# Matmul and DMA prices of a build-time scheduler, changed to the durations in the trace

## The chip, the cores and the metric

The kernel runs on one core of one Trainium2 chip. The metric is the device time of one execution in microseconds (us). TensorE is called PE here, VectorE DVE, ScalarE ACT, GpSimd POOL and SyncE SP. SP and POOL mainly issue DMA transfers.

## What is computed

The reference is a two-layer trunk over 528 tokens (16 learned meta tokens in front of 512 others), width 1024, all in float32. Cut to what matters:

```python
for l in range(DEPTH):                                   # DEPTH = 2
    n = rms_norm(h, mix_norm_g[l])
    # n @ w_in[l] is split by columns into q, k, v, qi, ki, wi (attention),
    # xr, yg (recurrent branch), c (convolution branch) and the merge gates
    logits = einsum("bqhd,bsd->bqhs", qi, ki)            # the indexer, 8 heads of 64
    iscore = einsum("bqhs,bqh->bqs", relu(logits), wi)
    _, sel = lax.top_k(iscore, 128)                      # each query keeps 128 keys
    p = softmax(q @ ksel * scale); o = p @ vsel          # 8 heads of 128, 2 key heads
    # recurrent branch: 4-tap conv, gates, scan, gelu
    # conv branch: GLU, 31-tap causal depthwise conv, layer norm, silu
    # three output projections, merge by sigmoid gates, w_out, residual
    # rms norm, SwiGLU feed-forward (2816 wide), residual
```

## The kernel before

**Tiles and passes.** Activations lie transposed in SBUF, as tiles `s` of 128 channels by 528 tokens. A product in float32 is made of three passes in a rounded format: weights and activations are each split into a rounded part (hi) and the rest (lo). `gemm` (from L539) first multiplies the hi weights with the activations' hi and lo (L568, the hi pass), then the lo weights with the activations' hi (L578, the lo pass). One output tile of 128 channels takes 32 matmuls of 264 columns at L568 and 16 at L578 in layer 0, and half as many of 512 columns in most of layer 1. The feed-forward and one projection use a scheme of seven products (`seven`, L609 and L613).

**The way of a weight.** SP loads 512 KB of raw weights (L397). ACT writes the rounded hi copy into a `w` slot, later a negated lo copy into another, and POOL issues a DMA that adds the raw weights from memory onto it (L400, `add_dma`). There are four `w` slots.

**The stages of a layer.** The norm; the product for the values (`v_gemm`, L891), whose first matmuls reuse a PSUM bank that DVE reads into `rtok` (L386, the reciprocal norms by token, used by the indexer); the indexer (`choose`), whose top-k runs on DVE as 16 rounds of MAX and MATCH_REPLACE over each of four score tiles (L1003 and L1004); rotations of q, k and the indexer's q (`rotate`: two POOL transfers that swap halves inside SBUF, s<-s, and three DVE operations at L379); then eight heads. A head is: scores on PE (L953, L962), a softmax (DVE at L1234, Exp on ACT, a reciprocal on DVE at L1237, a scaling on ACT), transposes of the probabilities on PE (L1325) and their product with the values (L1346). The 31 taps of the conv branch are DVE operations at L382 on tiles of about 512 elements; they need only their input tile. All through the stage the large products of the projection run on PE.

**What sets the order.** The kernel is written as some dozens of Python generators, and `Sched.run` (from L213) interleaves them when the program is built. Each yields an `Op` with an engine and a price in ns. `start` gives the time at which an op could start by the prices; `run` takes the op with the earliest start (within 40 ns by priority), emits it, and moves that engine's clock on. The outcome is one fixed queue of instructions for each engine, which the chip works through strictly in order, waiting on semaphores: the prices set an order and nothing else. A matmul's price is its columns over about 2.34 per ns; a transfer lands, by the plan, at the time its bytes have gone through a common pipe of 360 bytes per ns, plus `MOVE_LAT`, 1900 ns.

The names in the order's rows (`s_405`, `w_15414`) are numbered anew in each program; the text says which tiles they are.

Of the kernel before, what the change touches and what calls it, by code (L numbers as in the profile page):

```python
# [117 lines left out]
TABLES = {"Exp": ("e",), "Tanh": ("e", "g", "s"), "Gelu_apprx_tanh": ("g",), "Silu": ("s",), "Sqrt": ("q",),  # L118
          "Abs_reciprocal_sqrt": ("a",)}
TABLE_LOAD = 1283.0  # L120
MOVE_LAT = 1900.0
SELF = {"PE": 0.0, "DVE": 125.0, "ACT": 110.0, "SP": 0.0, "POOL": 0.0}
LAT = {"PE": 170.0, "DVE": 100.0, "ACT": 130.0, "SP": 0.0, "ACTQ": 0.0, "POOL": 0.0}

# [1 line left out]
class Sched:  # L126
# [80 lines left out]
    def run(self):  # L207
        while self.streams:
            moved = True
            while moved:  # L210
                moved = False
                for s in sorted(self.streams, key=lambda s: s[:2]):
                    r = s[3]  # L213
                    if isinstance(r, Box):
                        if r.done:
                            self.step(s, r.v)
                            moved = True
                            break
                    elif isinstance(r, Alloc) and r.kind in ("pp", "b1"):
                        b = self.bank(r.kind, r.keep)  # L220
                        if b is not None:
                            self.step(s, b)
                            moved = True
                            break
                    elif isinstance(r, Alloc):
                        free = self.slots[r.kind]
                        if len(free) >= r.n + (r.keep() if callable(r.keep) else r.keep):
                            got = []
                            for dt in r.dts:
                                at, i = heapq.heappop(free)  # L230
                                b = Buf(r.kind, i, self.make(r.kind, i, dt))
                                b.rd = at + 60.0
                                got.append(b)
                            self.step(s, got if r.many else got[0])
                            moved = True
                            break
            cands = []
            for s in self.streams:
                if isinstance(s[3], Op):
                    ready, t = self.start(s[3])  # L240
                    pen = max(0.0, TABLE_LOAD * (PEN_S if s[3].tab == ("s",) else PEN) - AGE * (t - ready)) if s[3].tab and self.table not in s[3].tab else 0.0
                    cands.append((t + pen, s, t))
            if not cands:
                if not self.streams:
                    return
                raise RuntimeError("nothing can go on: " + ", ".join(
                    f"{s[2].__name__}:{s[3].kind + str(s[3].n) if isinstance(s[3], Alloc) else 'box'}" for s in self.streams))
            first = min(cands, key=lambda c: c[0])
            e, until = first[1][3].eng, first[0] + WINDOW
            t0, s, t = min((c for c in cands if c[1][3].eng == e and c[0] <= until), key=lambda c: c[1][:2])  # L250
            op = s[3]
            cost = op.cost
            if op.tab:
                if self.table not in op.tab:
                    self.table = op.tab[0]
                    cost += TABLE_LOAD
            op.fn()
            end = t + cost
            self.clock[e] = end
            done = end  # L260
            if op.bytes:
                self.moved = max(self.moved, end + 650.0) + op.bytes / 360.0
                done = self.moved + MOVE_LAT
            for b in op.R:
                b.rd = max(b.rd, done + LAT[e])
            for b in op.W:
                b.ready, b.eng = max(b.ready, done), e
            self.step(s, None)
# [10 lines left out]
def trunk(ctx, tc, xT, wt, wv, wd, wg, gain_in, par_in, cst_in, id_in, out):  # L279
    nc = tc.nc  # L280
    V, S, PE = nc.vector, nc.scalar, nc.tensor
# [108 lines left out]
        return Op("DVE", cost, fn, R, W)  # L390

    def pe(cost, fn, R, W):
        return Op("PE", cost, fn, R, W)

    def dma(o, i, R, W, q="SP"):
        e = {"SP": nc.sync, "POOL": nc.gpsimd}[q]
# [157 lines left out]
    def gemm(wbox, nk, xs, cols, epi, prio, need="", keep=0, tail=0, ks=range(NF)):  # L554

        n = cols[1] * cols[2]
        bufs = (yield alloc(need, FT, keep)) if need else []
        hi = yield wbox[0]
        ps = yield psa(cols)
        cuts = [0, nk - tail, nk] if tail < nk else [*range(nk + 1)]  # L560
        for k0, k1 in zip(cuts[:-1], cuts[1:]):
            for k in ks[k0:k1]:
                xh, xl = yield xs[k]

                def go(k=k, xh=xh, xl=xl):
                    for i, b in enumerate((xh, xl)):
                        for o, x in by_part(ps, b, cols):
                            PE.matmul(o, hi[:, 128 * k:128 * k + 128], x, start=(k == ks[0] and i == 0), stop=False)  # L568
                yield pe(2 * n / 2.336, go, [hi, xh, xl], [ps])
            if k1 == nk and k0 < k1:  # L570
                free(hi)
            lo = yield wbox[1]
            for k in ks[k0:k1]:
                xh, _ = xs[k].v

                def go(k=k, xh=xh):
                    for o, x in by_part(ps, xh, cols):
                        PE.matmul(o, lo[:, 128 * k:128 * k + 128], x, start=False, stop=k == ks[nk - 1])  # L578
                yield pe(n / 2.336, go, [lo, xh], [ps])
        free(lo)  # L580
        spawn(epi(ps, psv(ps, cols), *bufs), prio)

    def seven(wb, qs, cols, epi, prio, need):
# [7 lines left out]
        for i in (1, 6, 2, 7, 5, 4, 3):  # L591
            wh, wl = yield wb[i]
            if i in (6, 5):
                pair[i] = pair[{6: 2, 5: 4}[i]] = yield Alloc("b1" if near else "pp")
            ps = pair[i] if i in pair else (yield Alloc("b1"))
            if i in pair:
                h = int(i in (6, 5))
                d = ps[:, h * n:h * n + n] if near else ps[:, h, :n]
            else:
                d = ps[:, :n]  # L600
            q = []
            for c in range(4):
                q.append((yield qs[c])[i])
            R = [t for x in q for t in x[:2]]

            def hi(w=wh, d=d, q=q):
                for c, (h, l, o) in enumerate(q):
                    for e, t in enumerate((h, l)):
                        PE.matmul(d, w[:, 128 * c:128 * c + 128], t[:, o:o + n], start=c == 0 and e == 0, stop=False)  # L609

            def lo(w=wl, d=d, q=q):
                for c, (h, l, o) in enumerate(q):
                    PE.matmul(d, w[:, 128 * c:128 * c + 128], h[:, o:o + n], start=False, stop=c == 3)  # L613
            yield pe(8 * n / 2.336, hi, R + [wh], [ps])
            yield pe(4 * n / 2.336, lo, R + [wl], [ps])
            free(wh, wl)
            done[i].set((ps, d))
# [1150 lines left out]
```

## Time and profile before

| | |
|---|---|
| median of three runs | 2175.06 us (2170.46 to 2175.31) |
| profiled execution | 2181.13 us, its span 2179.3 us |
| PE busy | 2103.5 us, 97% |
| DVE busy | 1587.6 us, 73% |
| ACT busy | 1364.8 us, 63% |
| mean granted PE clock | 0.991 of full |

PE is busy in all but some 76 us of the span, so the view to read is what PE waits for. The other engines have a lower share over the whole span, but not in every stretch: DVE's share is near 0.9 in the attention stages (about 78 to 360 us and 1165 to 1440 us) and lower elsewhere. Every time below is in us from the start of the span.

### The profile page before, as it was taken

To read this page: it belongs to the slowest core of one execution; us is meant where nothing else is said; L and a number is where in the kernel's file an instruction comes from. 1 tells how busy PE (TensorE), PEld (TensorE's weight loads), DVE (VectorE), ACT (ScalarE), POOL (GpSimd) and SP (SyncE) were. 2 spreads that over 40 slices of the span, in tenths; PEclk is the share of its full clock that TensorE was granted. 3 is DMA by queue.
4 is the path that set the end of the run, shared out by engine and by line. 5 is a ranking of instruction groups with operands and counts; after the bars stand their busy time and mean duration, and the time that the engine had idled before them with its cause. 6 is when DMAs were issued, how large, how long until landed. Compare 5 with 4: busy or idle time off the path is not lost.

```text
span 2179.3 us, 38132 instructions
## 1 busy us (share of the span) xinstructions
PE 2103.5 (97%) x14808; PEld 1974.2 (91%) x14808; DVE 1587.6 (73%) x2990; ACT 1364.8 (63%) x2113; POOL 318.4 (15%) x392
## 2 busy tenths in 40 slices
PE   6989999999999999999999899999999999999999
PEld 6889999999999999999989888988877887899997
DVE  7699987997237487677668999889972465767674
ACT  6556878876565465555457478888765645655452
POOL 1112110111111011111111111111111110111120
PEclk9999999999999999999999999999999999999999
DMA  8468654788887486576466686568888966766563
GB/s 229 101 142 187 144 120 104 172 175 170 174 202 184 120 184 148 131 169 165 103 186 144 148 186 138 122 133 170 181 178 182 214 156 140 181 151 158 148 143 107
DMA packets 127045, 342.68 MB, mean 157 GB/s; under 512 B 14864, under 2 KB 17040, under 8 KB 126864
## 3 DMA queue, kind: packets, MB, share of 16 engines
q0 software_dynamic: 50112, 145.47, 37.6%
q1 hardware_dynamic: 76608, 194.76, 30.7%
q8 instruction: 116, 1.90, 0.3%
q14 instruction: 65, 0.53, 0.1%
q10 hardware_dynamic: 144, 0.02, 0.0%
HBM read 327.91 MB, written 4.26 MB: 152 GB/s over the span
## 4 chain that ended last, share of the span: by engine, by line
PE 68%; DMA 14%; issue 10%; DVE 3%; ACT 3%; POOL 1%; POOLq 0%; DVEq 0%; ACTq 0%
PE banks L568 28%; PE banks L578 16%; DMA w<-in_wt_dram 14%; PE banks L609 11%; PE banks L613 6%; PE banks L1346 1%; PE banks L891 1%; DVE s L379 1%; PE banks L953 1%; PE banks L1325 1%; ACT w L376 1%; ACT s L376 1%; PE banks L962 1%; PE banks L1086 1%; DVE mx L1003 1%
## 5 line engine op out<-in xcount | busy, mean ns | idle before, releaser
L568 PE MATMUL banks<-s,w 128*128 128x264 f32 (+1 forms) x6432 | 1032.6, 313 | 12.8 <-ACT w L376 7.1
L568 PEld LDWEIGHTS banks<-s,w 128*128 128x128 f32 x6432 | 907.5, 190 | 80.8 <-ACT w L376 7.1
L376 ACT ACTIVATE w<-raw 128x1024 fp32r<-128x1024 f32 (+3 forms) x486 | 480.5, 993 | 338.9 <-PE banks L568 131.9
L578 PE MATMUL banks<-s,w 128*128 128x264 f32 (+1 forms) x3216 | 554.3, 317 | 34.0 <-DMA w<-in_wt_dram 33.5
L578 PEld LDWEIGHTS banks<-s,w 128*128 128x128 f32 x3216 | 463.5, 191 | 79.7 <-DMA w<-in_wt_dram 46.5
L376 ACT ACTIVATE s<-s 128x512 fp32r<-128x512 f32 (+8 forms) x640 | 379.7, 614 | 90.4 <-DVE s L379 68.3
L379 DVE TENSOR_TENSOR s<-s,s 128x528 f32<-128x528 f32 (+9 forms) x522 | 329.5, 656 | 59.2 <-ACT s L376 39.5
L379 DVE TENSOR_TENSOR s<-s,banks 128x512 f32<-128x512 f32 (+3 forms) x340 | 195.4, 588 | 225.2 <-PE banks L578 128.4
L400 POOL DMA_DIRECT2D w<-in_wt_dram x192 | 167.2, 871 | 1262.4 <-ACT w L376 1110.7
L382 DVE SCALAR_TENSOR_TENSOR s<-s,half,s 128x512 f32<-128x512 f32 (+22 forms) x480 | 344.0, 745 | 3.6 <-ACT s L376 0.3
L609 PE MATMUL banks<-s,s 128*128 128x264 f32 (+1 forms) x2464 | 346.0, 283 | 0.4 <-DVE s L379 0.3
L609 PEld LDWEIGHTS banks<-s,s 128*128 128x128 f32 x2464 | 317.9, 188 | 2.4 <-DVE s L379 0.8
L376 ACT ACTIVATE s<-banks 128x528 f32<-128x528 f32 (+11 forms) x338 | 165.0, 505 | 127.5 <-PE banks L578 49.0
L376 ACT ACTIVATE s<-u 128x512 fp32r<-128x512 f32 x176 | 110.5, 628 | 182.3 <-DVE u L379 167.1
L613 PE MATMUL banks<-s,s 128*128 128x264 f32 (+1 forms) x1232 | 199.0, 284 | 6.9 <-DMA s<-in_wt_dram 6.9
L400 POOL DMA_DIRECT2D s<-in_wt_dram x132 | 113.8, 862 | 514.1 <-ACT s L376 343.8
L613 PEld LDWEIGHTS banks<-s,s 128*128 128x128 f32 x1232 | 168.9, 188 | 8.7 <-DMA s<-in_wt_dram 7.5
L379 DVE TENSOR_TENSOR s<-u,s 128x512 fp32r<-128x512 f32 x176 | 119.8, 688 | 33.6 <-ACT s L376 31.0
L382 DVE SCALAR_TENSOR_TENSOR s<-s,banks 128x528 f32<-128x528 f32 (+1 forms) x48 | 33.4, 696 | 117.4 <-PE banks L578 117.3
L376 ACT ACT_TABLE_LOAD x80 | 102.6, 1283 | 4.9 <-DMA s<-in_xT_dram 3.6
L379 DVE TENSOR_TENSOR w<-raw,w 128x512 fp32r<-128x512 f32 (+2 forms) x94 | 75.5, 811 | 5.3 <-ACT w L376 4.4
L379 DVE TENSOR_TENSOR u<-s,s 128x512 f32<-128x512 f32 x88 | 60.3, 686 | 24.5 <-DMA s<-in_wt_dram 24.5
(128 smaller groups left out, 1278.9 us busy)
## 6 DMA issues: line engine op xcount, KB each, us to landing
raw<-in_wt_dram SPq DMA_DIRECT2D x206, 512.0 KB, 4.3
w<-in_wt_dram POOLq DMA_DIRECT2D x192, 512.0 KB, 7.7
s<-in_wt_dram SPq DMA_DIRECT2D x176, 256.0 KB, 5.0
s<-in_wt_dram POOLq DMA_DIRECT2D x132, 256.0 KB, 4.5
raw<-in_wd_dram SPq DMA_DIRECT2D x64, 256.0 KB, 3.7
raw<-in_wd_dram SPq DMA_DIRECT2D x16, 384.0 KB, 3.8
s<-s POOLq DMA_DIRECT2D x36, 132.0 KB, 7.3
s<-in_xT_dram SPq DMA_DIRECT2D x16, 264.0 KB, 4.8
```

What stands on the lines that cost most here:

```text
L376: return Op("ACT", cost, lambda: S.activation(o, i, f, **kw), R, W, TABLES.get(name))
L379: return Op("DVE", 69 + width(o) / 0.96, lambda: V.tensor_tensor(o, a, b, op), R, W)
L382: return Op("DVE", (69 if isinstance(s, float) else 129) + width(o) / 0.96, lambda: V.scalar_tensor_tensor(o, a, s, b, op0, op1), R, W)
L400: return Op("POOL", 1040.0, lambda: nc.gpsimd.dma_start(out=o, in_=i, accum_op=ALU.add), R, W, None, 4 * o.shape[0] * width(o))
L568: PE.matmul(o, hi[:, 128 * k:128 * k + 128], x, start=(k == ks[0] and i == 0), stop=False)
L578: PE.matmul(o, lo[:, 128 * k:128 * k + 128], x, start=False, stop=k == ks[nk - 1])
L609: PE.matmul(d, w[:, 128 * c:128 * c + 128], t[:, o:o + n], start=c == 0 and e == 0, stop=False)
L613: PE.matmul(d, w[:, 128 * c:128 * c + 128], h[:, o:o + n], start=False, stop=c == 3)
L891: PE.matmul(ps[:tn, :264], a[:, t0:t0 + tn], b[:, o:o + 264], start=e + part + k == 0 and a is nh, stop=bool(e and part and k == 3))
L953: PE.matmul(ps[:, :w], a, b[:, :w], start=e == 0, stop=e == n - 1)
L962: PE.matmul(ps[:, c, :hw], a, b[:, c * hw:(c + 1) * hw], start=e == 0, stop=e == n - 1)
L1003: yield dve(70 + w / 0.96, lambda: V.max(mx[rows], sv[rows]), [sc], [])
```

## The change

Two prices of the plan are replaced. A transfer's price now depends on the queue that issues it: bytes per ns and a fixed latency of (310, 2000) for SP and ACT, and (210, 4300) for POOL, in place of 360 and 1900 for all. The price of every PE op is multiplied by 1.066. Prices of DVE and ACT operations, of issuing a DMA (470 ns on SP, 1000 or 1040 on POOL) and all else stay. The set of instructions is the same but for one ACT table load more (81 for 80). Line numbers after L261 are one higher in the changed kernel.

```diff
-MOVE_LAT = 1900.0
+MOVE = {"SP": (310.0, 2000.0), "ACTQ": (310.0, 2000.0), "POOL": (210.0, 4300.0)}
@@ Sched.run
             if op.bytes:
-                self.moved = max(self.moved, end + 650.0) + op.bytes / 360.0
-                done = self.moved + MOVE_LAT
+                rate, lat = MOVE[op.eng]
+                self.moved = max(self.moved, end + 650.0) + op.bytes / rate
+                done = self.moved + lat
@@ 
     def pe(cost, fn, R, W):
-        return Op("PE", cost, fn, R, W)
+        return Op("PE", 1.066 * cost, fn, R, W)
```

**First place: DVE before the value product of layer 0.** Before, the queue reads as follows up to `rtok`; s_405 to s_408 and s_485 to s_488 belong to the rotations of the last two tiles of the indexer's q, s_600 to s_612 to the norm.

```order
68 L379 TENSOR_TENSOR s_405<-s_405,s_130 128x528
69 L379 TENSOR_TENSOR s_406<-s_406,s_134 128x528
70 L379 TENSOR_TENSOR s_612<-s_610,s_611 128x528
71 L379 TENSOR_TENSOR s_405<-s_405,s_406 128x528
72 L379 TENSOR_TENSOR s_485<-s_485,s_130 128x528
73 L379 TENSOR_TENSOR s_486<-s_486,s_134 128x528
74 L379 TENSOR_TENSOR s_407<-s_405,s_407 64x528
75 L379 TENSOR_TENSOR s_408<-s_405,s_408 64x528
76 L379 TENSOR_TENSOR s_485<-s_485,s_486 128x528
77 L386 TENSOR_SCALAR rtok<-banks 128x4
```

In the changed program the same stretch reads as follows; the two rotations are now s_411 to s_414 and s_496 onward, and the norm's last tile is s_588 and s_590.

```order
66 L380 TENSOR_TENSOR s_320<-s_318,s_320 64x528
67 L387 TENSOR_SCALAR rtok<-banks 128x4
68 L340 SCALAR_TENSOR_TENSOR sp_p<-sp_p,sp_y 128x16
69 L380 TENSOR_TENSOR s_590<-s_588,s_589 128x528
70 L380 TENSOR_TENSOR s_321<-s_318,s_321 64x528
71 L340 SCALAR_TENSOR_TENSOR sp_p<-sp_p,sp_y 128x16 x5
72 L341 SCALAR_TENSOR_TENSOR sp_p<-sp_p,sp_z 128x16
73 L342 TENSOR_SCALAR sp_m<-sp_m 128x16
74 L343 SCALAR_TENSOR_TENSOR sp_p<-sp_p,sp_m 128x16
75 L344 TENSOR_SCALAR s4p<-sp_p 128x16
76 L345 TENSOR_SCALAR s4n<-sp_p 128x16
77 L380 TENSOR_TENSOR s_411<-s_411,s_130 128x528
```

`rtok` has moved from row 77 to row 67, ahead of both rotations and of the split of the norm's last tile.

**Second place: PE at head 0 of layer 1.** Before, the transposes of head 0 (u_14562 is one of its probability tiles) stand behind half of the hi pass of w_15451; the whole lo pass of w_15414 lies ahead of that.

```order
6287 L568 MATMUL banks<-s_13327,w_15451 128x264 x2
6288 L568 MATMUL banks<-s_13328,w_15451 128x264 x2
6289 L568 MATMUL banks<-s_13347,w_15451 128x264 x2
6290 L568 MATMUL banks<-s_13348,w_15451 128x264 x2
6291 L568 MATMUL banks<-s_13375,w_15451 128x264 x2
6292 L568 MATMUL banks<-s_13376,w_15451 128x264 x2
6293 L568 MATMUL banks<-s_13396,w_15451 128x264 x2
6294 L568 MATMUL banks<-s_13397,w_15451 128x264 x2
6295 L962 MATMUL banks<-s_13662,s_14682 128x264 x2
6296 L962 MATMUL banks<-s_13663,s_14682 128x264 x2
6297 L962 MATMUL banks<-s_13662,s_14683 128x264 x2
6298 L1325 MATMUL banks<-ident,u_14562 128x128
```

In the changed program w_15419 is the hi half of the weights whose lo half was w_15414 before, and u_14597 is the tile of probabilities.

```order
6269 L1210 MATMUL banks<-ones,s_15288 128x1 x4
6270 L569 MATMUL banks<-s_13378,w_15419 128x264 x2
6271 L569 MATMUL banks<-s_13379,w_15419 128x264 x2
6272 L569 MATMUL banks<-s_13411,w_15419 128x264 x2
6273 L569 MATMUL banks<-s_13412,w_15419 128x264 x2
6274 L963 MATMUL banks<-s_13662,s_14695 128x264 x2
6275 L963 MATMUL banks<-s_13663,s_14695 128x264 x2
6276 L963 MATMUL banks<-s_13662,s_14696 128x264 x2
6277 L1326 MATMUL banks<-ident,u_14597 128x128
```

The transposes now stand inside the hi pass of the product before: 4 hi matmuls of it, its lo pass of 16, 16 hi matmuls of the next one and eight small sums (L1209) have gone from ahead of them to behind them.

**Third place: DVE at the softmax of the same head.** Before, the last reciprocal of head 0 (st_15537, of the tile with 528 columns) is row 1843.

```order
1838 L1234 ISA s_14559,st_15537<-banks,s_13726,qr 128x528
1839 L1234 ISA st_15537 128x1
1840 L379 TENSOR_TENSOR s_15352<-s_15352,s_15354 128x512
1841 L382 SCALAR_TENSOR_TENSOR s_15523<-s_14380,half,s_15523 128x512
1842 L1211 COPY msq<-banks 128x4
1843 L1237 RECIPROCAL st_15537<-st_15537 128x1
```

In the changed program the same reciprocal is st_15500, in row 1860; s_14343 and s_15216 are conv tiles, as s_15523 above.

```order
1849 L383 SCALAR_TENSOR_TENSOR s_15216<-s_14386,half,s_15216 128x512
1850 L383 SCALAR_TENSOR_TENSOR s_14343<-s_14140,half,s_14343 128x509
1851 L383 SCALAR_TENSOR_TENSOR s_15216<-s_14386,half,s_15216 128x512
1852 L380 TENSOR_TENSOR s_15287<-s_15287,s_12857 128x512
1853 L380 TENSOR_TENSOR s_15289<-s_15289,s_12863 128x512
1854 L1238 RECIPROCAL st_15384<-st_15384 128x1
1855 L1235 ISA s_14594,st_15500<-banks,s_13726,qr 128x528
1856 L1235 ISA st_15500 128x1
1857 L380 TENSOR_TENSOR s_15287<-s_15287,s_15289 128x512
1858 L383 SCALAR_TENSOR_TENSOR s_15216<-s_14386,half,s_15216 128x512
1859 L1212 COPY msq<-banks 128x4
1860 L1238 RECIPROCAL st_15500<-st_15500 128x1
```

Between the value product of layer 1 and this reciprocal stand 19 conv taps that stood behind it before, and four operations of a rotation and a split (L379) that stood ahead have gone behind it.

## Rows read from the trace of the kernel before

**Rows 1.** What PE waits for: engine, line, waited for, us in total, times, longest.
```profile
PE banks L578 <- DMA w<-in_wt_dram: 33.5, 30, 3.9
PE banks L891 <- DVE rtok L386: 13.7, 1, 13.7
```

**Rows 2.** Timeline of PE: start, us, engine, line, operation, idle before and releaser.
```profile
44.87 1.22 PE L891 MATMUL banks<-w,s 128*128 128x264 f32 x8
59.82 15.48 PE L891 MATMUL banks<-w,s 128*128 128x264 f32 x112 [13.73 <-DVE rtok L386]
```

**Rows 3.** Timeline of DVE around `rtok` in layer 0.
```profile
53.69 6.00 DVE L379 TENSOR_TENSOR s<-s,s 128x528 f32<-128x528 f32 x9
59.61 0.15 DVE L386 TENSOR_SCALAR rtok<-banks 128x4 f32<-128x4 f32 x1
74.25 0.41 DVE L379 TENSOR_TENSOR vmeta<-banks,vmeta 16x256 fp32r<-16x256 f32 x1 [12.09 <-ACT vmeta L376]
```

**Rows 4.** Windows: stretch, length, busy PE, PEld, DVE, ACT, POOL (instructions), PE clock, DMA, GB/s.
```profile
59.80:63.40 3.60, 3.58 (x16) 3.58 (x17) 2.15 (x7) 1.27 (x2) 0.00 (x0) 0.50 0.00 0
63.40:67.00 3.60, 3.60 (x32) 3.60 (x31) 0.00 (x0) 1.06 (x1) 0.00 (x0) 1.00 0.00 0
```

**Rows 5.** Timeline of PE around a lo pass in layer 0.
```profile
706.64 4.07 PE L568 MATMUL banks<-s,w 128*128 128x264 f32 x32
710.55 2.11 PE L578 MATMUL banks<-s,w 128*128 128x264 f32 x16
718.17 2.23 PE L578 MATMUL banks<-s,w 128*128 128x264 f32 x16 [1.60 <-DMA w<-in_wt_dram]
```

**Rows 6.** Timeline of ACT: the lo copy for the wait at 718.17.
```profile
708.77 1.04 ACT L376 ACTIVATE w<-raw 128x1024 fp32r<-128x1024 f32 x1
```

**Rows 7.** DMA issues of the page: out<-in, engine, count, KB each, us to landing.
```profile
w<-in_wt_dram POOLq DMA_DIRECT2D x192, 512.0 KB, 7.7
s<-in_wt_dram POOLq DMA_DIRECT2D x132, 256.0 KB, 4.5
s<-s POOLq DMA_DIRECT2D x36, 132.0 KB, 7.3
```

**Rows 8.** Timeline of PE at the transposes: head 1 of layer 0, head 0 of layer 1.
```profile
265.54 0.60 PE L1346 MATMUL banks<-s,s 128*128 128x256 f32 x3
265.98 0.49 PE L1325 MATMUL banks<-ident,u 128*128 128x128 f32 x3
...
1337.16 0.95 PE L1209 MATMUL banks<-ones,s 128*128 128x1 f32 x8
...
1338.54 2.12 PE L568 MATMUL banks<-s,w 128*128 128x264 f32 x16
...
1341.22 0.49 PE L1325 MATMUL banks<-ident,u 128*128 128x128 f32 x3
```

**Rows 9.** Timeline of ACT: the last softmax scalings ahead of those transposes.
```profile
264.83 0.74 ACT L376 ACTIVATE s<-s,st 128x528 f32<-128x528 f32 x1
...
1340.28 0.73 ACT L376 ACTIVATE s<-s,st 128x528 f32<-128x528 f32 x1
```

**Rows 10.** Timeline of DVE ahead of head 0 of layer 1.
```profile
1338.80 0.16 DVE L1237 RECIPROCAL st<-st 128x1 f32<-128x1 f32 x1
1338.87 0.74 DVE L382 SCALAR_TENSOR_TENSOR s<-s,half,s 128x512 f32<-128x512 f32 x1
```

**Rows 11.** Windows from the value products to the first heads, columns as in rows 4.
```profile
78.00:258.00 180.00, 173.26 (x1370) 170.66 (x1368) 165.71 (x408) 125.68 (x183) 31.47 (x42) 0.98 0.71 159
1165.00:1341.00 176.00, 165.98 (x1112) 154.50 (x1111) 158.57 (x382) 118.81 (x175) 31.16 (x42) 0.97 0.70 158
```

**Rows 12.** What DVE waits for from 1165 to 1339, columns as in rows 1.
```profile
DVE s L379 <- DMA s<-s: 5.6, 5, 1.8
```

**Rows 13.** Timeline of DVE: one cycle of the top-k on two score tiles.
```profile
1194.80 0.30 DVE L1004 MATCH_REPLACE8 u<-mx,u 64x144 f32<-64x144 f32 x1
...
1196.62 0.30 DVE L1004 MATCH_REPLACE8 u<-mx,u 64x144 f32<-64x144 f32 x1
```

## The prediction

> **What bounds the kernel now.** I read the page's busy shares first, then what PE waits for, then the timelines of PE, DVE and ACT at each of those waits, and last the order of both programs. PE is busy all but 76 us of the span, so a new order can only touch those 76 us or add to them. Two entries lead [rows 1]: 30 short waits for lo weights, 33.5 us together, and one wait of 13.7 us in which the value product of layer 0 stands until DVE has read a bank into `rtok`. PE was through with the first eight matmuls of that product at 46.1 and went on at 59.82 [rows 2]; DVE reached `rtok` at 59.61, behind nine operations of 6.00 us, and once it was past the next few it stood idle for 12.1 us until the product was done [rows 3]. So there a few microseconds of rows in DVE's queue cost PE as much.
>
> In the attention stages two engines are near their limit: from the value product to the first heads PE is busy 173 of 180 us and 166 of 176, DVE 166 and 159 [rows 11]. There the transposes on PE come right behind the last scaling on ACT: in layer 1 the scaling of head 0 ends at 1341.01 and the transposes start at 1341.22; for head 1 of layer 0 it is 265.57 and 265.98 [rows 8, 9]. PE does not wait there now, but it has 0.2 to 0.4 us to spare.
>
> **The new prices against the trace.** 32 matmuls of 264 columns take 3.91 us from start to start [rows 5], 122 ns each. The old price is 113, the new one 120.5: it is right now. A POOL transfer of 512 KB was planned to land 0.65 + 1.46 + 1.9 = 4.0 us after its issue, now 0.65 + 2.5 + 4.3 = 7.4; the page says 7.7 [rows 7]. One of 256 KB is now planned at 6.2 and takes 4.5, one of a swap at 5.6 and takes 7.3. What stays wrong is DVE's top-k: two MAX and two MATCH_REPLACE on tiles of 144 and 272 are priced 2 x 220 + 2 x 353 = 1147 ns, and the cycle takes 1.82 us [rows 13]. Over 16 rounds the plan has DVE some 11 us early, by these two tiles alone. The old price of PE had PE early as well, by 6.6% of 166 us, 11 us [rows 11]. The two errors were about equal, and this is why the transposes met the softmax so closely. One of them is now gone.
>
> The Trainium skill, "TensorE: Matmul & The Clock Gate", section "Wait — 56ns, not 53.3ns?", gives back-to-back matmuls N / 2.4 GHz plus some 2.5 ns, which is an estimate of 112.5 ns for 264 columns. By that rule the old price was right, and the new one would plan PE 7% too slow. The trace disagrees, with 122 ns in rows 5.
>
> **Term 1, the value product of layer 0.** `rtok` moves ahead of the nine rows that ran from 53.69 (6.0 us) and of one 64-row operation more (0.7): 6.7 us. All of this has room behind it, in the 12.1 us that DVE is idle [rows 3]. Some small operations also go behind it, but before they ran while DVE was idle anyway. What could be late next is the norm's own chain between ACT and DVE, which had the nine rows as cover: it could take back a microsecond or two. I take -7, between -5 and -8.3. PE then waits 6 to 7 us in place of 13.7. PE ran at half the clock for the first 3.6 us after that wait, 16 matmuls where the next 3.6 us have 32 [rows 4], a loss of 1.8. A wait of 6 us will very likely still bring that; if not, up to -1.8 more.
>
> **Term 2, heads of layer 1.** PE reaches the transposes of head 0 with 36 matmuls and one group of eight sums less ahead of it: 36 x 0.122 + 0.95 [rows 8], 5.3 us. The softmax on DVE has 19 conv taps more ahead, each 0.65 us from start to start [rows 10], and four operations of about 0.6 us less: +10 us. DVE is idle 17 us of that stretch [rows 11], 5.6 of them waiting for swaps [rows 12], and taps depend on nothing late, so they can fill that. If exactly the idle time takes them, the softmax is where it was and PE waits 5.3 - 0.2 = 5.1; if none is filled, 15; if all is, about nothing. Heads 1 to 3 have 6 to 8 us less PE work ahead and 8 to 11 more on DVE, the same picture. I take +6, between 0 and +15.
>
> **Term 3, heads of layer 0.** At head 1, 72 matmuls, a group of sums and ten rows of the values' product (0.2 us each) have gone behind the transposes: 8.8 + 0.95 + 2.0, about 12 us. DVE's work ahead of the softmax is the same within 1 us. With DVE's times unchanged PE waits 11.6; with all of its 14.3 us of idle time filled, nothing. Earlier in the stage taps have moved ahead by 5 to 15 us, so half of that is likely filled: I take +5, between 0 and +12.
>
> **Term 4, waits for weights.** In the pure product stretches the order on PE and ACT is nearly word for word the same, so most of the 33.5 us stays: the wait at 718.17, say, comes from a lo copy at 708.77 that stands two operations back in ACT's queue [rows 5, 6], and these stand there still. Where PE now waits for a softmax, the transfers catch up meanwhile: some 2 us of the waits in the two attention stages go. I take -2, between -5 and +5.
>
> **Sum.** -7 + 6 + 5 - 2 = +2 us on the profiled execution's 2181.1, that is 2183. The median of the runs shown is 6.1 lower, so 2177. What a measurement can tell from no change is about 0.3%, 6.5 us: below 2168.5 it is faster, above 2181.6 slower.
>
> The same page of the Trainium skill, in Part 1 on the clock gate, says that the array is throttled by default and that activity releases it. The trace agrees with 16 against 32 matmuls in rows 4. By that rule each new wait in one piece of some microseconds would cost up to 1.8 us on top.
>
> **Rivals.**
>
> *The gain stays.* DVE fills nearly all of its idle time with taps, and the softmax comes as much sooner as the transposes do. Then terms 2 and 3 are 1 or 2 us each, and with them go waits for weights and the 1.8 of half clock: -7 + 3 - 5 - 1 = -10, 2165. For it: the taps are free to run in the waits for swaps, which the new price knows. Against it: the top-k price, which leaves DVE later than planned however its idle time is used.
>
> *Slower: the queues lock.* DVE's waits (swaps, ACT, banks) don't go but move, as each tap put ahead delays the next chain that PE, POOL or ACT needs. Then PE pays the full price at the heads: -7 + 12 + 15 - 3 = +17, 2192; I set 2190, as part is always filled. It decides from the point where less than half of DVE's 14 to 17 us is filled. For it: PE's queue is in order, so one late softmax stops the large products behind it as well; and ten times the tap's 0.65 us ahead of one softmax is more than PE has to spare. Against it: waits for swaps are a third of DVE's idle time, and they now have work in them.
>
> *The early `rtok` brings nothing*, since the chain of ACT and DVE behind the norm is the bound: term 1 is -1 at most, and the sum is +8, 2183 to 2185.
>
> **How the numbers follow.** The forecast, 2169 to 2184 about 2177, has 0.46: 0.38 of it within 0.3%, 0.05 slower, 0.03 faster. The gain stays: 0.26, of which 0.24 faster and 0.02 within. The queues lock: 0.20, of which 0.18 slower. Nothing from `rtok`: 0.08, of which 0.06 slower. That makes faster 0.27, within 0.44, slower 0.29. The range for 8 in 10 goes from the rival below to the one above, 2163 to 2192.
>
> **What would show it.** In what PE waits for: the wait of L892 for `rtok` at 5 to 8 us in place of 13.7; new waits of L1326 for ACT or DVE at heads 0 to 3 of both layers, some 5 us a layer; L579 for DMA still near 30 us. In what DVE waits for: swaps (s<-s) down. I am wrong if L1326 shows no wait, if PE waits in the heads for over 20 us, or if the wait for `rtok` stays above 11.

## The result, and the profile after

The changed kernel takes 2187.31 us (median of 4 runs, 2184.16 to 2189.66), the kernel before 2174.22 in the same comparison: a ratio of 1.0062, 95% interval 1.0042 to 1.0083. It is slower by 0.6%. The forecast was 2177, the range 2163 to 2192, with 0.29 for slower.

The profiled execution's span is 2187.7 us, 8.4 more than before. The medians are 13.1 apart: the profiled execution of before is 6.9 above its median, that of the change 2.2, so the traces show some 5 us less of the loss than the medians do. What PE waits for in it, with the columns of [rows 1]:

```profile
PE banks L579 <- DMA w<-in_wt_dram: 39.0, 31, 5.5
...
PE banks L610 <- DVE s L380: 5.8, 4, 2.2
PE banks L614 <- DMA s<-in_wt_dram: 5.3, 7, 1.7
PE banks L610 <- ACT s L377: 3.6, 2, 2.2
PE banks L963 <- ACT s L377: 3.5, 3, 1.5
PE banks L1210 <- ACT s L377: 2.8, 2, 1.6
PE banks L892 <- DVE rtok L387: 1.7, 1, 1.7
```

At the same hi products, the kernel before has:

```profile
PE banks L609 <- DVE s L379: 0.3, 1, 0.3
```

Against [rows 1] the wait for `rtok` has gone from 13.7 us to 1.7, and waits for weights have grown from 33.5 to 39.0. New are 9.4 us at L610 (L609 before), the hi products of the scheme of seven, for DVE and ACT, 3.5 us at L963, which fall in the indexer's stretches, and 2.8 us at L1210, the sums of squares of q at the heads of layer 1. L1326, the transposes, has no row.

PE's timeline at the value product of layer 0, to compare with [rows 2] (the view ends at 62, inside the last row's batch):

```profile
43.71 3.67 PE L579 MATMUL banks<-s,w 128*128 128x264 f32 x16 [3.83 <-DMA w<-in_wt_dram]
47.17 1.07 PE L866 MATMUL banks<-ones,s 128*128 128x1 f32 x8
48.10 1.22 PE L892 MATMUL banks<-w,s 128*128 128x264 f32 x8
51.01 11.17 PE L892 MATMUL banks<-w,s 128*128 128x264 f32 x78 [1.69 <-DVE rtok L387]
```

PE goes on at 51.01 in place of 59.82: 8.8 us gained. It comes to the product 3.2 us later than before (48.10 for 44.87), because it has waited 3.83 us for a lo weight and ran the 16 matmuls behind that wait in 3.67 us, for 2.12 before (granted clock 0.54 from 43.7 to 47.3). This costs nothing, since DVE reaches `rtok` later still.

DVE's timeline there, to compare with [rows 3]:

```profile
50.06 0.70 DVE L380 TENSOR_TENSOR s<-s,s 64x528 fp32r<-64x528 f32 x1
50.79 0.16 DVE L387 TENSOR_SCALAR rtok<-banks 128x4 f32<-128x4 f32 x1
```

The rotations that stood ahead of `rtok` have gone behind it. So the start gained, and yet the end came later. To see where, I take the start of the same matmul in the traces of two kernels and subtract. The table does this for the change and for each experiment below: microseconds against the kernel before, negative where the kernel is ahead. The columns are times in the trace of before: the second batch of the value product of layer 0; a lo pass after the heads of layer 0; the value product of layer 1; the first product after its heads; a product early in its feed-forward; the last matmul. Single executions of one kernel differ by a few microseconds, so a column says little by itself; the difference between two columns of a row is what counts. Even that has a spread: e4 has the prices of before up to the fourth column, and its row moves by 2.1 us from the third to the fourth.

| kernel | 59.8 | 437.1 | 1150.5 | 1485.9 | 1889.5 | 2174.9 |
|---|---|---|---|---|---|---|
| the change | -8.8 | -7.2 | -8.1 | -6.8 | -0.7 | +8.6 |
| e1 matmul price only | -1.8 | +8.3 | +11.1 | +20.1 | +18.3 | +18.3 |
| e2 transfer prices only | -8.7 | -10.4 | -15.6 | -14.5 | -13.8 | -7.6 |
| e3 new, then old | -9.4 | -5.4 | -7.1 | -5.5 | -8.8 | -8.4 |
| e4 old, then new | -0.2 | -0.7 | -0.9 | +1.2 | +4.2 | +13.2 |
| e5 change, 256 KB price old | -9.6 | -7.4 | -5.3 | -2.3 | -0.7 | -0.8 |
| e6 only the 256 KB price new | +1.4 | +1.6 | -1.7 | -1.8 | +3.9 | +11.8 |
| e7 e2, 256 KB price old | -7.9 | -10.0 | -10.0 | -8.8 | -11.5 | -10.9 |
| e8 e1 and top-k price | -3.1 | -2.6 | -3.6 | -5.4 | -5.3 | -5.3 |
| e9 e7 and top-k price | -8.9 | -15.5 | -18.2 | -22.7 | -27.7 | -27.4 |
| e10 e5 and top-k price | -9.5 | -14.0 | -14.3 | -25.7 | -24.4 | -24.1 |
| e11 256 KB price as the trace | -8.7 | -5.5 | +0.7 | +5.2 | +8.0 | +9.4 |
| e12 top-k price only | +1.1 | -8.7 | -7.8 | -18.4 | -17.3 | -17.4 |

The first row is the finding. The change is 7 to 9 us ahead through both attention stages, and loses 15.4 us after the heads of layer 1, 9.3 of them in the feed-forward (last two columns).

One of the new waits there, in PE's timeline:

```profile
2078.93 1.14 PE L610 MATMUL banks<-s,s 128*128 128x256 f32 x8
2079.91 0.63 PE L614 MATMUL banks<-s,s 128*128 128x256 f32 x4
2082.71 1.21 PE L610 MATMUL banks<-s,s 128*128 128x256 f32 x8 [2.17 <-DVE s L380]
```

DVE's timeline of the changed kernel at that place:

```profile
2078.05 0.69 DVE L380 TENSOR_TENSOR w<-raw,w 128x512 fp32r<-128x512 f32 x1 [0.35 <-ACT w L377]
2078.66 0.68 DVE L380 TENSOR_TENSOR u<-s,s 128x512 f32<-128x512 f32 x1
2079.38 0.69 DVE L380 TENSOR_TENSOR u<-u,s 128x512 f32<-128x512 f32 x1
2080.77 0.69 DVE L380 TENSOR_TENSOR s<-u,s 128x512 fp32r<-128x512 f32 x1 [0.70 <-ACT s L377]
2081.37 0.68 DVE L380 TENSOR_TENSOR u<-s,s 128x512 f32<-128x512 f32 x1
2081.98 0.68 DVE L380 TENSOR_TENSOR s<-s,banks 128x512 f32<-128x512 f32 x1
```

And DVE's timeline of the kernel before at the same products:

```profile
2076.17 0.69 DVE L379 TENSOR_TENSOR w<-raw,w 128x512 fp32r<-128x512 f32 x1 [0.61 <-ACT w L376]
2076.78 0.68 DVE L379 TENSOR_TENSOR u<-s,s 128x512 f32<-128x512 f32 x1
2077.38 0.68 DVE L379 TENSOR_TENSOR s<-s,banks 128x512 f32<-128x512 f32 x1
2077.98 0.69 DVE L379 TENSOR_TENSOR u<-u,s 128x512 f32<-128x512 f32 x1
```

The row `s<-s,banks` reads a finished product out of its bank, and PE needs that bank: it goes on at 2082.71, as this row ends at 2082.66. The rows that write or read `u` form sums of the *next* weights and split them. Before, one such row stood between the split of a weight (`w<-raw,w`) and the bank's row; now there are four, and one of them waits 0.70 us for ACT besides.

### The profile page after: what moved, and what is told of

The parts are those of the page before. It is cut to its first block, busy times and chain, and to the rows that moved or that the text cites. A ratio compares the mean times of both kernels' runs of the same rounds, so it can differ in the third digit from the quotient of the medians.

```text
span 2187.7 us, 38168 instructions
## 1 busy us (share of the span) xinstructions
PE 2111.2 (97%) x14808; PEld 1975.0 (90%) x14808; DVE 1585.5 (72%) x2990; ACT 1363.3 (62%) x2114; POOL 318.7 (15%) x392
## 5 line engine op out<-in xcount | busy, mean ns | idle before, releaser
L377 ACT ACTIVATE s<-s 128x512 fp32r<-128x512 f32 (+7 forms) x640 | 382.0, 615 | 149.7 <-DVE s L380 105.0
L380 DVE TENSOR_TENSOR s<-s,s 128x528 f32<-128x528 f32 (+8 forms) x522 | 329.8, 653 | 57.5 <-ACT s L377 46.7
L610 PE MATMUL banks<-s,s 128*128 128x264 f32 (+1 forms) x2464 | 349.1, 284 | 9.7 <-DVE s L380 5.8
L610 PEld LDWEIGHTS banks<-s,s 128*128 128x128 f32 x2464 | 319.9, 190 | 13.6 <-DVE s L380 6.7
```

The source lines that it names most:

```text
L377: return Op("ACT", cost, lambda: S.activation(o, i, f, **kw), R, W, TABLES.get(name))
L380: return Op("DVE", 69 + width(o) / 0.96, lambda: V.tensor_tensor(o, a, b, op), R, W)
```

## The experiments

All were compared with the kernel before, run on the same chip in between. Ratios are given with their 95% intervals.

**e1 and e2: the two prices apart.** The edits, to the kernel before and to the changed one:

```diff
-        return Op("PE", cost, fn, R, W)             # e1, in before
+        return Op("PE", 1.066 * cost, fn, R, W)
-        return Op("PE", 1.066 * cost, fn, R, W)     # e2, in the change
+        return Op("PE", cost, fn, R, W)
```

> Only the matmul price is new (x1.066); transfers keep the old price. Before is 2174, the full change 2187. If the loss comes from the matmul price (PE planned at its true speed, so that the rows which empty its banks are planned later and stand behind other work), this is at 2183 to 2190. If it comes from the transfer prices, it is at 2165 to 2176, with the gain at the value product of layer 0 if that one comes from the matmul price.

> Only the transfer prices are new; the matmul price is the old one. If the loss comes from the transfer prices, 2183 to 2190; if from the matmul price, 2165 to 2176. The wait for rtok, 13.7 us before and 1.7 with the full change, tells which of the two moved rtok.

e1 took 2196.07 us, a ratio of 1.0073 (1.006 to 1.0087). e2 took 2177.98, 0.9996 (0.9981 to 1.0011). Taken alone the matmul price costs 0.7%, and the transfer prices are level. Neither time lies in a stretch that was expected: e1 is 6 us above the first, and e2 lies between its two. The wait for `rtok` is 10.9 us in e1 and 4.7 in e2: it was mostly the transfer prices that moved `rtok`. But the table shows two different losses. e1 loses at the heads (10 us to the second column, 9 from the third to the fourth) and nothing later. e2 is ahead until the heads of layer 1 are through and loses in the feed-forward, 6 us; behind those heads it has 7.5 us of waits at L610, and e1 has none there.

**e3 and e4: where the loss is.** New prices up to a point in the plan's own clock of PE, old ones from there on (e3), and the other way round (e4). The point is the one that is 1485.9 in the table.

```diff
+CUT = 1452e3                                        # e4: 1333.6e3, and >=
-                rate, lat = MOVE[op.eng]
+                rate, lat = MOVE[op.eng] if self.clock["PE"] < CUT else (360.0, 1900.0)
-        return Op("PE", 1.066 * cost, fn, R, W)
+        return Op("PE", (1.066 if sch.clock["PE"] < CUT else 1.0) * cost, fn, R, W)
```

> New prices up to the end of the heads of layer 1 (1486 us in the trace of before), old prices from there on. The traces of before and after show the changed kernel 6.9 us ahead at that point and 8.6 behind at the end. Theory A (the loss is made after that point, by the order of DVE and ACT in the projections and the feed-forward of layer 1): 2165 to 2170, about 7 below before. Theory B (the loss is made in the attention stages, as the prediction had it, and the late part is only spread of the runs): 2178 to 2188.

> Old prices up to the same point, new ones from there on. Theory A: all of the loss and none of the gain, 2183 to 2192. Theory B: 2172 to 2178, as before.

e3 took 2173.08 us, 0.9977 (0.9966 to 0.9988); e4 2194.5, 1.0063 (1.0046 to 1.0081). Theory A holds: the new prices gain a little where I had looked for the loss, and lose all of it after the heads of layer 1. e3's median is 3 us above the expected stretch, but so is before's in these runs (2177.61, where the stretch was put against 2174); e4's is 2.5 us above its own. What PE waits for at the hi products of seven (L611 here) in e4, and in e3:

```profile
PE banks L611 <- DVE s L381: 5.6, 5, 2.1
PE banks L611 <- ACT s L378: 3.6, 2, 2.2
```

```profile
PE banks L611 <- DVE s L381: 0.2, 1, 0.2
```

**e5 to e7: which price it is.** The feed-forward's weights, in the scheme of seven, come in pieces of 256 KB. POOL's transfers of that size were planned at 3.3 us after the issue, and are planned at 6.2 in the change; the page of both kernels has them at 4.5 [rows 7].

```diff
                 rate, lat = MOVE[op.eng]             # e5 in the change, e7 in e2
+                if op.eng == "POOL" and op.bytes == 4 * 128 * 512:
+                    rate, lat = 360.0, 1900.0
-                self.moved = max(self.moved, end + 650.0) + op.bytes / 360.0   # e6, in before
+                rate, lat = (210.0, 4300.0) if op.eng == "POOL" and op.bytes == 4 * 128 * 512 else (360.0, MOVE_LAT)
+                self.moved = max(self.moved, end + 650.0) + op.bytes / rate
```

> The full change, but the POOL transfers of 256 KB (the lo halves of the feed-forward's weights, 4.5 us from issue to landing in the trace) are back at the old price, 3.3 us after the issue in place of 6.2. Theory P (the late loss comes from that price: the plan has the lo halves land 1.7 us later than they do, so it plans the products and the rows that empty their banks late, behind work for the next weights): the waits of the first line of seven (L610 in the changed kernel) for DVE and ACT, 9.4 us with the full change, go below 4, and the time is 2174 to 2181 against 2177 of before. Theory Q (the late loss comes from the price of the 512 KB transfers or of SP's): L610 still waits 8 us or more, 2185 to 2192.

> The kernel before with one price changed: POOL transfers of 256 KB at the new price. Theory P: rtok waits 13.7 us as before, nothing is gained early, and the waits of the first line of seven for DVE and ACT appear in the late part, 6 us or more; 2183 to 2190. Theory Q: 2174 to 2179, no such waits.

> The transfer prices of the change without the matmul price, and POOL's 256 KB at the old price. Theory P: the early gain of e2 (some 8 us at rtok) stays and the late waits go: 2163 to 2170, faster than before and than the change. Theory Q: as e2, about 2177.

e5 took 2175.05 us, 0.9994 (0.9981 to 1.0007); e6 2187.7, 1.0045 (1.0029 to 1.006); e7 2168.58, 0.9953 (0.9936 to 0.9971). All three are as theory P had them. What PE waits for at L612 in e5, at L610 in e6 and at L612 in e7:

```profile
PE banks L612 <- DVE s L382: 1.2, 2, 0.9
```

```profile
PE banks L610 <- DVE s L380: 7.9, 6, 2.2
PE banks L610 <- ACT s L377: 2.4, 3, 1.8
```

```profile
PE banks L612 <- DVE s L382: 1.4, 2, 0.9
```

The last two columns of the table say the same. In the feed-forward of layer 1 the four kernels that plan the late part with the new 256 KB price lose 9.3, 6.2, 9.0 and 7.8 us (the change, e2, e4, e6); the eight that plan it with the old one lose between -0.1 and 0.6. The transfers themselves take 4.5 us with either price (the change, e4, e6 and e7). How the price does it is argued, not shown, as no run gives the plan's own times: with the price too high the plan has the lo weights land late, so it has PE late, and orders the rows that empty PE's banks behind work for the next weights; on the chip PE is there earlier and waits.

**e8 and e12: the top-k price.** The prices of MAX and MATCH_REPLACE, put to the trace [rows 13], with the new matmul price (e8) and with no other edit (e12):

```diff
-                yield dve(70 + w / 0.96, lambda: V.max(mx[rows], sv[rows]), [sc], [])
-                yield dve(70 + w / 0.96, lambda: V.match_replace(sv[rows], mx[rows], sv[rows], TAKEN), [sc], [sc])
+                yield dve(190 + w / 0.96, lambda: V.max(mx[rows], sv[rows]), [sc], [])
+                yield dve(285 + w / 0.96, lambda: V.match_replace(sv[rows], mx[rows], sv[rows], TAKEN), [sc], [sc])
```

> The matmul price alone (e1, 0.7% slower) with the price of DVE's top-k put to the trace as well: MAX at 190 + w/0.96 and MATCH_REPLACE at 285 + w/0.96 ns in place of 70 + w/0.96. The trace of e1 loses 8 us between 230 and 262 and some 10 between 1341 and 1410, at the heads. If that is because the plan has DVE too early there (the prediction's account of why the heads lose), these go, and the time is 2175 to 2184. If the top-k price has no part in it, 2190 to 2197.

> The kernel before with the top-k price alone put to the trace; matmul and transfer prices old. The prediction's account (the matmul's and the top-k's errors cancelled in before, so correcting one alone loses): 2180 to 2190, with PE waiting at the heads or DVE's other rows late. The other account (a top-k price that is too low costs by itself, whatever the matmul price, as the step from e7 to e9 hints): 2160 to 2171.

e8 took 2173.78 us, 0.9979 (0.9961 to 0.9997), where e1 had 1.0073; e12 took 2160.3, 0.9928 (0.9906 to 0.9951). e8 is a microsecond below its expected stretch. So e1's loss at the heads does hang on the top-k price: in the stretch in which e1 loses most in layer 0, PE's windows in e1 and then in e8 are

```profile
225.00:265.00 40.00, 35.41 (x253) 34.24 (x253) 35.18 (x88) 31.36 (x59) 5.99 (x9) 0.91 0.52 120
```

```profile
225.00:265.00 40.00, 38.91 (x298) 36.95 (x297) 38.60 (x89) 33.09 (x63) 6.92 (x10) 1.00 0.55 126
```

PE is busy 3.5 us more and its clock is full (0.91 before that). But my account of it falls with e12: the old matmul price and the old top-k price did not cancel. The top-k price alone gives 15 us, under the old matmul price. Where it gains is the indexer's stretch, shown by the windows of before and then of e12:

```profile
100.00:150.00 50.00, 43.88 (x325) 42.91 (x323) 45.63 (x126) 29.10 (x37) 7.56 (x10) 0.93 0.62 137
1185.00:1245.00 60.00, 52.61 (x369) 50.70 (x368) 55.76 (x164) 29.34 (x37) 8.43 (x11) 0.91 0.65 148
```

```profile
100.00:150.00 50.00, 50.00 (x402) 49.61 (x401) 45.18 (x131) 34.75 (x42) 8.42 (x11) 1.00 0.78 172
1185.00:1245.00 60.00, 59.70 (x419) 56.05 (x418) 51.12 (x149) 34.01 (x41) 11.27 (x15) 1.00 0.84 183
```

In the first of the two, before has a wait of 2.66 us for a weight and one of 3.46 for DVE, with a lower clock behind them; e12 has none. Over the whole kernel the waits for lo weights are 21.6 us in e12, for 33.5 in before. The prediction had put the first kind down as waits for weights, and had not asked what else stood in the queues there.

**e9 to e11: put together.** e9 is e7 and e10 is e5, each with the top-k price of e8. e11 is the change with POOL's transfers priced by size:

```diff
                 rate, lat = MOVE[op.eng]
+                if op.eng == "POOL":
+                    rate, lat = 360.0, 3100.0 if op.bytes == 4 * 128 * 512 else 5400.0
```

> e7 (transfer prices new except POOL's 256 KB, matmul price old; 0.47% faster than before) with the top-k price put to the trace. If the gains add up, the heads give some 3 to 8 us more: 2160 to 2166. If the old matmul price and the old top-k price have to go together, since their errors cancel, it is no better than e7: 2167 to 2178.

> e5 (the full change with the old price for POOL's 256 KB; level with before) with the top-k price put to the trace. Here the matmul and the top-k price are both those of the trace. If the top-k price was what cost in the heads, 2165 to 2171; if the waits for weights decide (43.6 us in e5), 2173 to 2180.

> The full change with POOL's transfers priced by size as the trace has them: 256 KB at 0.65 + 0.73 + 3.1 = 4.5 us, the others at 360 bytes per ns and 5.4 us more (512 KB: 7.5). If a price that is right is enough for the late part, L610's waits for DVE and ACT are below 4 us and the time is 2172 to 2180; if it takes a price that is too low, as before, they stay at 6 us or more and the time is 2181 to 2190.

e9 took 2154.16 us, 0.99 (0.9879 to 0.9922), and is the best of all: 1.6% below the change. e10 took 2158.11, 0.9915 (0.9889 to 0.9941). The top-k price gives 0.5 to 0.9% in all four pairs (before and e12, e1 and e8, e7 and e9, e5 and e10). Both came out below what was expected.

e11 took 2189.9, 1.0067 (1.0044 to 1.0089): slow, as its second case had it, but not for that case's reason. What PE waits for in it:

```profile
PE banks L581 <- DMA w<-in_wt_dram: 48.3, 40, 6.9
...
PE banks L612 <- DVE s L382: 1.0, 1, 1.0
```

With a 256 KB price that is right, L612 waits 1.0 us and the feed-forward loses 1.4: a right price is enough there. The time is lost before it, from the first column to the fifth and most from the second to the fourth, with the most waits for weights of any kernel here. The 512 KB and swap prices of e11 differ from the change's too, and which of them does that was not tried.

**The matmul price in all pairs.** Five pairs of kernels differ in the matmul price alone. By their ratios to before, the new price is slower in each: by 0.7% alone (before and e1), 0.7% beside the new transfer prices (e2 and the change), 0.4% beside those with the old 256 KB price (e7 and e5), 0.5% beside the new top-k price (e12 and e8) and 0.15% beside both (e9 and e10; this last lies within the intervals). The 256 KB price costs 0.4 to 0.7% in its three pairs (before and e6, e7 and e2, e5 and the change). So it is not the whole of the loss: the change without it is level with before (e5), and faster than before only without the new matmul price as well (e7). A kernel with every price as in the trace, top-k included, was not run.

## Why the prediction came out as it did

The range held the time, but the forecast of "no change" did not: the sum was +2 us and the medians are 13 apart. The upper end of the range, 2192, was set for queues that lock at the heads, which they did not; that the time lies below it is in part luck. By its terms:

- **Term 1, the value product of layer 0: right, a little small.** -7 was forecast, between -5 and -8.3; -8.8 came. It is DVE's gain, as described: `rtok` starts at 50.79 for 59.61. The wait itself went to 1.7 us and not to 6 or 7, because PE came 3.2 us late, from a wait for a lo weight that the prediction had not seen. The 512 KB, swap and SP prices made the gain, for the most part, and not the 256 KB price (-7.9 in e7, -1.8 in e1, +1.4 in e6).
- **Terms 2 and 3, the heads: too large, and not by the mechanism described.** +6 and +5 were forecast; the table has +1.3 (third to fourth column) and +1.6 (first to second), within the spread that e4 shows. By the prediction's own sign it is wrong here, since L1326 waits for nothing. Its own condition says why: if all of DVE's idle time is filled, "about nothing" is left. That idle time was 14.3 and 17.4 us in the stretches of [rows 11]; in the changed kernel it is 5.3 and 4.9, and DVE no longer waits for swaps there. The windows of the change, set 8 us earlier:

```profile
70.00:250.00 180.00, 168.55 (x1337) 165.68 (x1337) 174.68 (x428) 122.21 (x184) 30.70 (x42) 0.99 0.69 155
1157.00:1333.00 176.00, 164.53 (x1098) 152.61 (x1097) 171.06 (x402) 120.72 (x178) 30.35 (x41) 0.97 0.70 157
```

What PE does wait for is 2.8 us at L1210 for ACT. A loss of some 10 us a stage appears in e1, where the matmul price stands alone, but not at the transposes either: e1 has no wait at L1325.

- **Term 4, the waits for weights: the step that failed.** "In the pure product stretches the order on PE and ACT is nearly word for word the same, so most of the 33.5 us stays" left out DVE, and it left out the scheme of seven, whose hi products wait for banks that DVE and ACT empty; such waits stood at nothing in the sum, without a reason. There DVE's rows had moved, as the two timelines show. The prediction had even noted that the 256 KB price was now 1.7 us too high, and drew nothing from it. After the heads of layer 1 the change lost 15.4 us, where -2 was forecast for all waits for weights, with bounds of -5 and +5. 9.3 of them are in the feed-forward from the fifth column on, 5.3 us of that as waits at L610. For the other 6 the trace has two more such waits, in the projection that uses the scheme of seven and in the first products of the feed-forward:

```profile
1753.86 1.91 PE L610 MATMUL banks<-s,s 128*128 128x256 f32 x8 [2.18 <-ACT s L377]
1876.39 1.63 PE L610 MATMUL banks<-s,s 128*128 128x256 f32 x8 [1.96 <-DVE s L380]
```

The waits for lo weights themselves went from 33.5 to 39.0; in the two attention stages they rose from 13.5 to 17.2, where 2 us less was forecast. e3 and e4 show the place of the loss, e5 to e7 that the 256 KB price makes its part in the feed-forward, and the trace the queue.

- **The rivals.** The first, in which the gain stays, has the course up to the end of the heads of layer 1: DVE fills most of its idle time, and terms 2 and 3 are 1 or 2 us each. It had nothing of the loss behind them. The slower one had the right kind of cause, a queue on which rows for later work stand ahead of those that PE waits for, but the wrong stage.
- **The account of two errors that cancel** was argued from sizes alone (11 us each) and is refuted by e12.

Open is why the feed-forward of layer 0, with the same prices, loses nothing (the change stands at -7.2 before it and -8.1 after). The products of layer 1 have 256 columns a half in place of 264, and the code gives two of them one bank there; whether that is the reason was not tried. Open, too, is how much of the 6 us between 1485.9 and 1889.5 the two waits make: e2, e4 and e6 have 3.3, 4.0 and 4.5 us of waits at this line there, and lose 0.7, 2.9 and 5.7. And where the matmul price costs in the change, beside the transfer prices, was not followed up.

## What to carry to other kernels

A list scheduler's price is worth what it does to the order of the queues that the bound engine waits for; a price that is nearer the trace on average can still be wrong for one size of transfer, and that size can cost more than the others gain. A right price need not pay by itself: the matmul price, now as in the trace, cost in all pairs, and with POOL's prices nearer the trace by size e11 was slower than before. Compare every price with the trace by size and not by kind, change one at a time, and read the moved rows on every engine, above all the rows that empty the bound engine's banks. The largest error left in a table is not always the one that is being mended: here it was two DVE operations, worth 15 us.

## What had not been expected of the hardware

POOL's accumulating transfers of 256 KB land in 4.5 us and those of 512 KB in 7.7, but its swaps of 132 KB inside SBUF take 7.3 in before and 6.2 to 7.3 in the kernels here: on that queue time does not go with bytes. In the indexer's stretches of e12, PE's mean clock is 1.00 where before has 0.93 and 0.91. In before, the granted clock was 0.51 from 131.7 to 135.1, behind the wait of 3.46 us, so part of such a wait's price is paid after it. Shorter waits could go either way: in the change it was 0.53 from 1753.9 to 1757.5 and 0.58 from 1876.4 to 1880.0, behind waits of 2.18 and 1.96 us, and 1.00 from 2082.7 to 2086.3, behind one of 2.17 us.
